# Two trunk layers: state-space tables begun inside the prologue, the first gate vector on TensorE, a pause in the modulation

## The chip, the cores and the metric

The kernel runs on one core of one Trainium2 chip. The metric is the device time of one execution in microseconds, taken as the median over runs; the profile is one further execution of the same program, recorded by the hardware profiler. The engines are TensorE (PE, with its weight loads as PEld), VectorE (DVE), ScalarE (ACT), GpSimd (POOL) and SyncE (SP), which here only starts transfers.

## The reference

Five blocks of 128 tokens (128 context tokens, 512 latent tokens) of width 1024 go through two layers. Cut to what matters here:

```python
def trunk_layer(h, cond, p, ctx):
    m = modulation(cond, p["w_mod"], p["b_mod"])          # silu(cond) @ w_mod + b_mod, 9 vectors of 1024
    sh1, sc1, g1, sh2, sc2, g2, sh3, sc3, g3 = [m[:, :, j] for j in range(N_MOD)]
    x = rmsnorm(h, p["norm_ffn1"]) * (1 + sc1) + sh1
    h = h + 0.5 * g1 * swiglu(x, p["ffn1_w_gate"], p["ffn1_w_up"], p["ffn1_w_down"])
    x = rmsnorm(h, p["norm_mix"]) * (1 + sc2) + sh2
    mixed, new_ctx = token_mixing(x, p, ctx)              # S5 scan | banded attention | axial attention | DFT
    h = h + g2 * mixed
    x = rmsnorm(h, p["norm_ffn2"]) * (1 + sc3) + sh3
    h = h + 0.5 * g3 * swiglu(x, p["ffn2_w_gate"], p["ffn2_w_up"], p["ffn2_w_down"])
```

swiglu is silu(x @ wg) * (x @ wu) @ wd with a hidden width of 2816. The S5 part of token_mixing needs, from parameters alone, the powers of a = exp(lambda dt) and matrices made of b and c; these are the "SSM tables". All of it is float32.

## The kernel before

**Work and tiling.** h is held transposed (`hT`, channels on the partitions) in two halves: half 0 has 256 columns (context and the first latent block), half 1 has 384. A float32 product is made of three matmuls on split operands: `whi` (a rounded copy of the weights, ACT, L205) and `wlo` (the rest, DVE, L206), `xh` and `xl` likewise for x. So a weight slab `raw` of 1 MB costs a transfer on SP's queue (L188), two ACT and two DVE operations, and then three matmuls for each 128 x 128 block.

**Prologue.** `load_x` loads the tokens and starts the first modulation slabs: shift sh1 and scale sc1 are wanted before anything else. `first_load(q)` starts two transfers of 1 MB (`wf`) for quarter q = 0 to 3 of scale (gi = 1) and shift (gi = 0); `first_mod(q)` multiplies each on PE (`macc`, L403, 8 instructions, each recorded twice in the trace's counts), copies it on ACT (`mev`, L406), transposes it on PE with a small matmul (`mpt`, L409) and adds the bias on DVE (`modT`, L411). Then `x_prep` makes xh and xl of blocks k = 2q and 2q + 1 (DVE L550 and L554, ACT L553, L557 and L559, POOL L560). The four of these rounds are called stages here, q0 to q3.

**First feed-forward part (FFN1).** Its hidden blocks f0 and f1 are computed together, k by k as x becomes ready (L663 to L665, 192 matmuls, called "the first 192" here); all later blocks go one at a time through `mm3` (L257 to L259), first gate and up (`gu`), then down (`y`). The residual is L592.

**Work beside it.** Two side streams are fed in by a count of modelled TensorE time, `tick`. (1) The rest of the modulation: `mod_step` makes one 512 KB slab (`wm`, started from POOL's queue, L347) into a partial sum with four DVE operations (`mvec`, L374 and L376); every four steps the partial sum is finished on PE (`macc` L422, four instructions), copied (`mev` L425) and transposed (`mpt` L432, two). Eight steps, so two such sums, make one vector of 1024; steps 0 to 15 would be those that the prologue makes in the other way, so the stream begins with steps 16 to 23 (the first gate g1) within 40 us of counted time, and steps 24 to 71 follow within 300 us. Two `wm` buffers rotate. (2) `ssm_tables`, a generator whose pieces are taken one by one: three pieces that only start 15 small transfers (`lamn`, `ldt`, `bn`, `cn`, `dcol`, `eye`), one with transposes on PE (`pl` L758, `pb` L764, `pc` L771), then many small DVE operations (`z`, `apow`, `eb`), transposes `ebT` (L952) and products `zt` (L973).

**What sets the order.** A scheduler fixes the order of each engine's instructions when the program is built; each engine then runs its own list in that order and waits at the first instruction whose operands are missing. Short-lived tiles (`mev`, `xt`, `rbs`, `lamn`, `cn`, `sg`, `hx`) share one pool of 5 buffers (tag "t"), and the two `rbs` tiles (the row factors) hold two of them through the prologue. By the waits in that order, a transfer of SP's queue starts when the eighth one before it has landed.

**Mixer entry.** At the end of FFN1 the squares of h are summed (`sq`, DVE L575; `pss`, PE L583), turned into 1/rms (`ms`, DVE L511; `rst`, POOL L512), spread over the partitions (`diag`, DVE L522; `rb`, PE L525), and x of the mixer is made from it in two halves. Half 0's S5 input is `pu`, the projections are `pj` (L1010 to L1012).

Of the kernel before, what the change touches and what calls it, by code (L numbers as in the profile page):

```python
# [36 lines left out]
T_OUT = 6500  # L37
FIN = 5
JOB_N = 2500
JOB_D = 12000  # L40
M_LAG = 3000
M_P0 = 40
M_P1 = 300
M_P2 = 340
X_PAT = ("dbdbdbdb", "dbbdbbdb")
LEAD = 2
# [59 lines left out]
class Net:  # L106
# [245 lines left out]
    def mod_step(self):  # L352


        nc = self.nc
        i = self.m_use
        if i == self.m_limit and self.mod_then:
            self.mod_to(*self.mod_then)
            self.mod_then = None
        if i >= min(len(self.mseq), self.m_limit):  # L360
            return
        self.m_use += 1
        l, gi, k = self.mseq[i]
        self.mod_load(i + 1)
        slab = self.mslab.pop(i)
        kk = k % 4
        if kk == 0:
            self.mvec = self.modp.tile([P, 2, 512], F32, name="mvec", tag="mvec")
        for j in range(2):
            w = slab[:, j * 512:(j + 1) * 512]  # L370
            for v in range(2):
                c = self.cs[:, 2 * kk + j, v:v + 1]
                if kk == 0 and j == 0:
                    nc.vector.tensor_scalar(self.mvec[:, v], w, c, None, op0=OP.mult)  # L374
                else:
                    nc.vector.scalar_tensor_tensor(self.mvec[:, v], w, c, self.mvec[:, v], op0=OP.mult, op1=OP.add)  # L376
        self.mod_load(i + 1 + self.mod_bufs)
        if kk == 3:
            mv = self.mvec
            self.later(M_LAG, lambda: self.mod_sum(l, gi, k // 4, mv))  # L380
        if not self.m_pace:
            self.tick(0)
# [33 lines left out]
    def mod_sum(self, l, gi, h, mv):  # L416
# [8 lines left out]
        nc.scalar.activation(ev[:, 0:256], acc, AF.Copy)  # L425
        self.later(900, lambda: self.mod_fin2(l, gi, h, ev))

    def mod_fin2(self, l, gi, h, ev):
        nc = self.nc
        pt = self.b([P, 2, P], name="mpt")  # L430
        for q in range(2):
            nc.tensor.transpose(pt[:, q, :], ev[:, q * P:(q + 1) * P], self.ident)  # L432
        src = pt.rearrange("p q (v s m) -> p v s q m", v=2, s=2)
        k0 = gi * 8 + h * 4
        dst = self.modT[l][:, k0:k0 + 4, :].rearrange("p (s q) v -> p s q v", s=2)
        bias = self.bmod[:, l, k0:k0 + 4].rearrange("p (s q) -> p s q", s=2)
        for v in range(2):
            nc.vector.tensor_tensor(dst[:, :, :, v], src[:, v, :, :, 0], bias, op=OP.add)
        if h == 1:
            self.mod_done(l, gi)  # L440

    def mod_to(self, n, ns=None):

        self.m_limit = n
        if ns is not None:
            self.m_pace = ns / max(n - self.m_use, 1)
            self.m_ns = self.m_pace
            return
        self.m_pace = None
        while self.m_use < n:  # L450
            self.mod_step()
# [26 lines left out]
    def load_x(self):  # L478
        nc, a = self.nc, self.a
        self.rs_tok = self.per.tile([P, 5], F32, name="rs_in", tag="rst", bufs=2)  # L480
        ss = self.per.tile([P, 5], F32, name="ss_in", tag="ss", bufs=2)
        xin = [self.xp.tile([P, w // P, D], F32, name=f"xin{i}", tag=f"xh{i}") for i, (_, w) in enumerate(HALVES)]
        junk = self.xp.tile([P, 2, D], F32, name="sqj", tag="xl0")
        xt = [xin[0][:, i] for i in range(2)] + [xin[1][:, i] for i in range(3)]
        for i in range(5):
            src = a["x_prompt"][0] if i == 0 else a["x_sample"][0, (i - 1) * P:i * P, :]
            nc.sync.dma_start(out=xt[i], in_=src)
        vecs = self.setup_vectors()
        next(vecs)
        self.load_limit = 2  # L490
        self.first_load(0)
        self.load_upto(2)
        self.first_load(1)
        for i in range(5):
            nc.scalar.activation(junk[:, i % 2], xt[i], AF.Square, accum_out=ss[:, i:i + 1])
            half = 0 if i < 2 else 1
            c0 = (i * P) - HALVES[half][0]
            for q in range(2):
                pt = self.b([P, 4, P], name="xT")
                for s in range(4):  # L500
                    nc.tensor.transpose(pt[:, s, :], xt[i][:, (4 * q + s) * P:(4 * q + s + 1) * P], self.ident)
                self.evac(self.hT[half][:, 4 * q:4 * q + 4, c0:c0 + P], pt)
        self.rstd_from(ss[:, 0:5], 0, 5)
        for _ in vecs:
            pass
# [1221 lines left out]
def build(tc, a, depth=DEPTH):  # L1727
    n = Net(tc, a, depth)
    nc = n.nc
    with ExitStack():  # L1730
# [14 lines left out]
        e_pro, pro = n.open_pool("pro", side="right")  # L1745
        n.open_ring_b()
        n.open_modp(2)
        n.load_x()
        rb = [n.norm_bc(h) for h in range(2)]
        for q in range(4):  # L1750
# [2 lines left out]
            n.first_mod(q)  # L1753
            for h in range(2):
                n.x_prep(h, 0, 0, rb[h], range(2 * q, 2 * q + 2))
        n.load_limit = n.seg[0][1]
        n.job = n.ssm_tables(pro, 0)
        n.job_ns = JOB_D
        n.e_mod.close()
        n.prep_to(4)  # L1760
# [1 line left out]
        for l in range(depth):  # L1762
            last = l + 1 == depth
            for j in (0, 2):
# [5 lines left out]
                    n.job = n.ssm_tables(pro, tab)  # L1770
                if l == 0 and j == 0:
                    n.mod_to(24, M_P0 * 1e3)
                    n.mod_then = (72, M_P1 * 1e3)
                else:
                    n.mod_to(min(72 * l + (72 if j == 0 else 96), 72 * depth), M_P2 * 1e3)
                n.ffn(l, j, (l, 1) if j == 0 else ((None, None) if last else (l + 1, 0)), chunks,
# [37 lines left out]
```

## Time and profile before

| | us |
|---|---|
| median of 3 runs (lowest, highest) | 2590.75 (2590.13, 2592.15) |
| the profiled execution: its time | 2590.19 |
| the profiled execution: its span | 2588.3 |
| PE busy | 2521.3 |
| DVE busy | 1499.7 |
| ACT busy | 831.6 |
| POOL busy | 375.4 |

Busy time counts every instruction but those that only branch, wait or start a transfer. The span runs from the first to the last instruction of the record; the 1.9 us between it and the execution's time lie around it. In rows of the timeline, the first number is the start, the second the duration, and the bracket behind a row says how long the engine had been idle and what it waited for; "SPq" rows are issues of transfers, in which the queue may wait too.

### The profile page before, as it was taken

Reading aid. Unit: us, or ns where it says so; the run is one execution under the profiler, and the core shown is the slowest. Engines: PE = TensorE matmul, PEld = TensorE weight load, DVE = VectorE, ACT = ScalarE, POOL = GpSimd, SP = SyncE. Lnnn points to the kernel's source line nnn. Section 1 sums busy time; section 2 is a strip of 40 time slices with the busy share of each in tenths; the row PEclk is TensorE's granted clock in tenths of the full one; section 3 lists DMA queues with packets and bytes.
Section 4 is the critical chain, followed back from the end, with each engine's and each line's share of the span. In section 5 each row is a group of like instructions: output and inputs, shape, how many; then the busy total and the mean of one; then the engine's idle time right before and its main releaser. Section 6 shows DMA issues by size and latency. Waiting matters only on the chain.

```text
span 2588.3 us, 41614 instructions
## 1 busy us (share of the span) xinstructions
PE 2521.3 (97%) x17082; PEld 2375.1 (92%) x17082; DVE 1499.7 (58%) x3014; ACT 831.6 (32%) x1570; POOL 375.4 (15%) x775
## 2 busy tenths in 40 slices
PE   7899999999899999999999999999999999999998
PEld 5799999998679899999999999999876799999998
DVE  5888676353667876454456666644446773333333
ACT  5232222242453532222233222223425553222222
POOL 2122010015701211000011001000183010000000
PEclk8899999999899999999999999999999999999999
DMA  8556454231104254343314445432401133221311
GB/s 270 151 172 192 137 156 146 90 98 55 37 26 147 66 168 127 109 126 98 115 50 152 134 127 153 136 100 66 125 19 54 34 99 98 68 84 62 98 49 41
DMA packets 205253, 273.94 MB, mean 106 GB/s; under 512 B 17224, under 2 KB 176680, under 8 KB 204552
## 3 DMA queue, kind: packets, MB, share of 16 engines
q1 hardware_dynamic: 183048, 193.30, 23.4%
q0 software_dynamic: 22016, 78.00, 10.0%
q8 instruction: 134, 2.20, 0.4%
q14 instruction: 55, 0.45, 0.1%
HBM read 256.29 MB, written 14.97 MB: 105 GB/s over the span
## 4 chain that ended last, share of the span: by engine, by line
PE 77%; issue 8%; POOL 7%; DVE 6%; DMA 2%; ACT 1%; SPq 0%; DVEq 0%; POOLq 0%; ACTq 0%
PE gu L257 14%; PE gu L259 14%; PE gu L258 14%; PE y L257 8%; PE y L258 8%; PE y L259 8%; POOL ee L1124 2%; POOL sc L1121 2%; POOL ee L1123 1%; POOL sc L1122 1%; DVE wlo L206 1%; DVE xt L550 1%; PE macc L422 1%; PE pj L1010 1%; PE pj L1011 1%
## 5 line engine op out<-in xcount | busy, mean ns | idle before, releaser
L257 PE MATMUL gu<-xh,whi 128*128 128x256 f32 (+1 forms) x2560 | 793.2, 310 | 0.9 <-DVE hx L676 0.9
L259 PE MATMUL gu<-xh,wlo 128*128 128x256 f32 (+1 forms) x2560 | 788.6, 308 | 0.6 <-DVE wlo L206 0.6
L258 PE MATMUL gu<-xl,whi 128*128 128x256 f32 (+1 forms) x2560 | 787.8, 308 | 0.0
L205 ACT ACTIVATE whi<-raw 128x1024 fp32r<-128x1024 f32 (+2 forms) x344 | 328.6, 960 | 881.5 <-PE gu L258 435.2
L206 DVE TENSOR_TENSOR wlo<-raw,whi 128x1024 fp32r<-128x1024 f32 (+2 forms) x344 | 377.0, 1098 | 347.3 <-ACT whi L205 346.8
L257 PEld LDWEIGHTS gu<-xh,whi 128*128 128x128 f32 x2560 | 480.6, 188 | 12.3 <-issue 10.2
L258 PEld LDWEIGHTS gu<-xl,whi 128*128 128x128 f32 x2560 | 481.7, 188 | 1.3 <-issue 1.2
L259 PEld LDWEIGHTS gu<-xh,wlo 128*128 128x128 f32 x2560 | 481.0, 188 | 2.0 <-issue 1.2
L257 PE MATMUL y<-hh,whi 128*128 128x384 f32 (+1 forms) x1408 | 435.6, 311 | 0.0
L259 PE MATMUL y<-hh,wlo 128*128 128x384 f32 (+1 forms) x1408 | 434.8, 309 | 0.0
L258 PE MATMUL y<-hl,whi 128*128 128x384 f32 (+1 forms) x1408 | 434.6, 309 | 0.1
L376 DVE SCALAR_TENSOR_TENSOR mvec<-wm,cs,mvec 128x512 f32<-128x512 f32 x448 | 316.7, 746 | 22.1 <-DMA wm<-in_w_mod_dram 21.7
L592 DVE SCALAR_TENSOR_TENSOR hT<-y,G,hT 128x128 f32<-128x128 f32 (+1 forms) x432 | 175.5, 436 | 229.1 <-PE y L259 228.9
L257 PEld LDWEIGHTS y<-hh,whi 128*128 128x128 f32 x1408 | 266.4, 190 | 3.3 <-issue 2.9
L258 PEld LDWEIGHTS y<-hl,whi 128*128 128x128 f32 x1408 | 267.5, 190 | 0.4 <-DVE hl L678 0.3
L259 PEld LDWEIGHTS y<-hh,wlo 128*128 128x128 f32 x1408 | 267.2, 190 | 0.0
L347 POOL DMA_DIRECT2D wm<-in_w_mod_dram x128 | 92.0, 718 | 939.4 <-DVE mvec L376 800.0
L676 DVE TENSOR_TENSOR hx<-sg,gu 128x256 f32<-128x256 f32 (+1 forms) x176 | 85.0, 483 | 121.4 <-ACT sg L674 121.1
L677 ACT ACTIVATE hh<-hx 128x256 fp32r<-128x256 f32 (+1 forms) x176 | 82.8, 471 | 187.4 <-DVE hx L676 187.3
L512 POOL TENSOR_TENSOR rst<-ms,mhalf 128x2 f32<-128x2 f32 (+1 forms) x12 | 11.2, 932 | 855.7 <-DVE ms L511 855.7
L674 ACT ACTIVATE sg<-gu 128x256 f32<-128x256 f32 (+1 forms) x176 | 75.3, 429 | 183.3 <-PE gu L259 176.5
L678 DVE TENSOR_TENSOR hl<-hx,hh 128x256 fp32r<-128x256 f32 (+1 forms) x176 | 86.2, 492 | 51.2 <-ACT hh L677 50.9
(311 smaller groups left out, 3238.4 us busy)
## 6 DMA issues: line engine op xcount, KB each, us to landing
wm<-in_w_mod_dram POOLq DMA_DIRECT2D x128, 512.0 KB, 4.1
raw<-in_ffn_w_gate_dram SPq DMA_DIRECT2D x44, 1024.0 KB, 5.4
raw<-in_ffn_w_up_dram SPq DMA_DIRECT2D x44, 1024.0 KB, 5.1
raw<-in_ffn_w_down_dram SPq DMA_DIRECT2D x24, 1024.0 KB, 5.1
raw<-in_ffn_w_down_dram SPq DMA_DIRECT2D x16, 768.0 KB, 4.6
raw<-in_w_in_dram SPq DMA_DIRECT2D x12, 1024.0 KB, 5.2
wf<-in_w_mod_dram SPq DMA_DIRECT2D x8, 1024.0 KB, 10.7
raw<-in_ffn_w_down_dram SPq DMA_DIRECT2D x16, 512.0 KB
```

The costliest lines, as they stand in the source:

```text
L205: self.nc.scalar.activation(hv, v, AF.Copy)
L206: self.nc.vector.tensor_tensor(lv, v, hv, op=OP.subtract)
L257: self.nc.tensor.matmul(out, wh, xh, start=(i == 0), stop=False)
L258: self.nc.tensor.matmul(out, wh, xl, start=False, stop=False)
L259: self.nc.tensor.matmul(out, wl, xh, start=False, stop=(i == n - 1))
L347: self.nc.gpsimd.dma_start(out=t.rearrange("p (j c) -> p j c", j=2), in_=w[kk * 256:(kk + 1) * 256, c0:c0 + 512].rearrange("(j p) c -> p j ...
L376: nc.vector.scalar_tensor_tensor(self.mvec[:, v], w, c, self.mvec[:, v], op0=OP.mult, op1=OP.add)
L592: nc.vector.scalar_tensor_tensor(h, y[:, s:e], G[:, k, v:v + 1], h, op0=OP.mult, op1=OP.add)
L674: nc.scalar.activation(sg[:, 0:w], g, AF.Silu)
L676: nc.vector.tensor_tensor(hx[:, 0:w], sg[:, 0:w], u, op=OP.mult)
L677: nc.scalar.activation(hh[half][:, f, :], hx[:, 0:w], AF.Copy)
L678: nc.vector.tensor_tensor(hl[half][:, f, :], hx[:, 0:w], hh[half][:, f, :], op=OP.subtract)
```

## The change

Three edits. **(a)** The table generator is created ahead of `load_x`. Its three pieces of transfers are issued right behind `first_load(1)`, its transposes behind stage q2, its next piece behind stage q3, and the first later piece is due after 5000 instead of 12000 counted ns. **(b)** Steps 16 to 23 of the modulation (`M_PE = 24`) are made on PE: 8 matmuls per step accumulate 128 columns each in one PSUM buffer over four steps (`macc`, L375 of the new program), then one copy, one transpose and one DVE addition (`mod_fin1`). **(c)** Steps 24 to 71 are spread over 360 instead of 300 counted us, and the first of them is due 60 us later (`M_D1`). At the end of FFN1 the line `n.mod_to(n.m_limit)` runs, as before, what is left of the steps.

```diff
--- before.py
+++ after.py
@@ -37,10 +37,12 @@
 T_OUT = 6500
 FIN = 5
 JOB_N = 2500
-JOB_D = 12000
+JOB_D = 5000
 M_LAG = 3000
 M_P0 = 40
-M_P1 = 300
+M_P1 = 360
+M_D1 = 60
+M_PE = 24
 M_P2 = 340
 X_PAT = ("dbdbdbdb", "dbbdbbdb")
 LEAD = 2
@@ -364,6 +366,22 @@
         self.mod_load(i + 1)
         slab = self.mslab.pop(i)
         kk = k % 4
+        if i < M_PE:
+            if kk == 0:
+                self.macc = self.b([P, P], name="macc")
+            for j in range(2):
+                for t in range(4):
+                    c0 = j * 512 + t * P
+                    nc.tensor.matmul(self.macc[32 * t:32 * t + 32, :], self.cs[:, 2 * kk + j, :], slab[:, c0:c0 + P],
+                                     start=(kk == 0 and j == 0), stop=(kk == 3 and j == 1), skip_group_check=True)
+            self.mod_load(i + 1 + self.mod_bufs)
+            if kk == 3:
+                ev = self.t(P, "mev")
+                nc.scalar.activation(ev[:, 0:P], self.macc, AF.Copy)
+                self.later(900, lambda: self.mod_fin1(l, gi, k // 4, ev))
+            if not self.m_pace:
+                self.tick(0)
+            return
         if kk == 0:
             self.mvec = self.modp.tile([P, 2, 512], F32, name="mvec", tag="mvec")
         for j in range(2):
@@ -425,6 +443,17 @@
         nc.scalar.activation(ev[:, 0:256], acc, AF.Copy)
         self.later(900, lambda: self.mod_fin2(l, gi, h, ev))
 
+    def mod_fin1(self, l, gi, h, ev):
+        nc = self.nc
+        pt = self.b([P, P], name="mpt")
+        nc.tensor.transpose(pt, ev[:, 0:P], self.ident)
+        src = pt.rearrange("p (t m) -> p t m", t=4)
+        k0 = gi * 8 + h * 4
+        nc.vector.tensor_tensor(self.modT[l][:, k0:k0 + 4, :], src[:, :, 0:2],
+                                self.bmod[:, l, k0:k0 + 4, None].to_broadcast([P, 4, 2]), op=OP.add)
+        if h == 1:
+            self.mod_done(l, gi)
+
     def mod_fin2(self, l, gi, h, ev):
         nc = self.nc
         pt = self.b([P, 2, P], name="mpt")
@@ -439,12 +468,12 @@
         if h == 1:
             self.mod_done(l, gi)
 
-    def mod_to(self, n, ns=None):
+    def mod_to(self, n, ns=None, delay=0):
 
         self.m_limit = n
         if ns is not None:
             self.m_pace = ns / max(n - self.m_use, 1)
-            self.m_ns = self.m_pace
+            self.m_ns = self.m_pace + delay
             return
         self.m_pace = None
         while self.m_use < n:
@@ -491,6 +520,8 @@
         self.first_load(0)
         self.load_upto(2)
         self.first_load(1)
+        for _ in range(3):
+            next(self.job)
         for i in range(5):
             nc.scalar.activation(junk[:, i % 2], xt[i], AF.Square, accum_out=ss[:, i:i + 1])
             half = 0 if i < 2 else 1
@@ -1745,6 +1776,7 @@
         e_pro, pro = n.open_pool("pro", side="right")
         n.open_ring_b()
         n.open_modp(2)
+        n.job = n.ssm_tables(pro, 0)
         n.load_x()
         rb = [n.norm_bc(h) for h in range(2)]
         for q in range(4):
@@ -1753,8 +1785,9 @@
             n.first_mod(q)
             for h in range(2):
                 n.x_prep(h, 0, 0, rb[h], range(2 * q, 2 * q + 2))
+            if q >= 2:
+                next(n.job)
         n.load_limit = n.seg[0][1]
-        n.job = n.ssm_tables(pro, 0)
         n.job_ns = JOB_D
         n.e_mod.close()
         n.prep_to(4)
@@ -1770,7 +1803,7 @@
                     n.job = n.ssm_tables(pro, tab)
                 if l == 0 and j == 0:
                     n.mod_to(24, M_P0 * 1e3)
-                    n.mod_then = (72, M_P1 * 1e3)
+                    n.mod_then = (72, M_P1 * 1e3, M_D1 * 1e3)
                 else:
                     n.mod_to(min(72 * l + (72 if j == 0 else 96), 72 * depth), M_P2 * 1e3)
                 n.ffn(l, j, (l, 1) if j == 0 else ((None, None) if last else (l + 1, 0)), chunks,
```

Three places in the order of instructions follow, of before and then of the changed program (whose line numbers are higher by 2 to 31).

SP's queue in the prologue, up to the transfers of stages q2 and q3 (`wf` x4), before:

```order
L188 DMA raw<-in_ffn_w_up_dram 128x8x256
L390 DMA wf<-in_w_mod_dram 128x8x256 x2
L732 DMA ldt<-in_ssm_log_dt_dram 64x16 x2
L751 DMA dcol<-in_ssm_d_dram 16x4x1 x4
L755 DMA eye_737<-in_k_eye_dram 128x16
L390 DMA wf<-in_w_mod_dram 128x8x256 x4
L188 DMA raw<-in_ffn_w_gate_dram 128x8x256
```

The same place after the change:

```order
L408 DMA wf<-in_w_mod_dram 128x8x256 x2
L758 DMA lamn<-in_ssm_lambda_re_dram 16x2x64
L758 DMA lamn<-in_ssm_lambda_im_dram 16x2x64
L763 DMA ldt<-in_ssm_log_dt_dram 64x16 x2
L769 DMA bn<-in_ssm_b_re_dram 16x2x1024
L769 DMA bn<-in_ssm_b_im_dram 16x2x1024
L775 DMA cn<-in_ssm_c_re_dram 128x2x64 x2
L775 DMA cn<-in_ssm_c_im_dram 128x2x64 x2
L782 DMA dcol<-in_ssm_d_dram 16x4x1 x4
L786 DMA eye_177<-in_k_eye_dram 128x16
L408 DMA wf<-in_w_mod_dram 128x8x256 x4
L190 DMA raw<-in_ffn_w_gate_dram 128x8x256
```

The `wf` x4 of stages q2 and q3 stood behind seven small transfers and now stands behind fifteen.

ACT's list in the prologue, before: `mev_394` is the second of stage q2 (`mev_378` stands just ahead of it), `mev_433` and `mev_449` to q3, `whi_637` and `whi_643` are the first copies of the gate and up slabs of f2 and f3:

```order
L406 ACTIVATE mev_394<-macc_385 128x256
L553 ACTIVATE xh0_284<-xt_400,modT0_96 128x128 x2
L557 ACTIVATE xt_407<-xt_407,modT0_96 128x128 x2
L557 ACTIVATE xt_414<-xt_414,modT0_96 128x384
L559 ACTIVATE xh0_284<-xt_407 128x256
L559 ACTIVATE xh1_300<-xt_414 128x384
L557 ACTIVATE xt_419<-xt_419,modT0_96 128x384
L406 ACTIVATE mev_433<-macc_424 128x256
L205 ACTIVATE whi_637<-raw_483 128x1024
L559 ACTIVATE xh1_300<-xt_419 128x384
L406 ACTIVATE mev_449<-macc_440 128x256
L205 ACTIVATE whi_643<-raw_489 128x1024
```

After the change `mev_400` and `mev_416` belong to q2, and `whi_832` and `whi_838` are those same copies:

```order
L590 ACTIVATE xh0_306<-xt_375 128x256
L588 ACTIVATE xt_382<-xt_382,modT0_96 128x384
L590 ACTIVATE xh1_322<-xt_382 128x384
L207 ACTIVATE whi_832<-raw_596 128x1024
L207 ACTIVATE whi_838<-raw_602 128x1024
L584 ACTIVATE xh1_322<-xt_387,modT0_96 128x384
L424 ACTIVATE mev_400<-macc_391 128x256
L424 ACTIVATE mev_416<-macc_407 128x256
L584 ACTIVATE xh0_306<-xt_422,modT0_96 128x128 x2
```

The copies of the f2 and f3 slabs stood among the evacuations of q3 and now stand ahead of those of q2.

DVE's list at the mixer entry, from the last squares to the x of half 1, before:

```order
L575 TENSOR_TENSOR sq_5069<-sq_5069,sqt 128x384 x2
L511 TENSOR_SCALAR ms<-pss 128x3
L522 TENSOR_SCALAR diag<-ident,rst 128x128 x3
L1591 TENSOR_SCALAR sink<-sink 128x4
L161 COPY uT<-pu 128x32x8
L550 SCALAR_TENSOR_TENSOR xt<-hT_71,A_2562,rbs 128x384 x4
```

And after the change:

```order
L606 TENSOR_TENSOR sq_4983<-sq_4983,sqt 128x384 x2
L542 TENSOR_SCALAR ms<-pss 128x3
L392 TENSOR_SCALAR mvec<-wm,cs 128x512 x2
L394 SCALAR_TENSOR_TENSOR mvec<-wm,cs,mvec 128x512 x14
L163 COPY uT<-pu 128x32x8
L553 TENSOR_SCALAR diag<-ident,rst 128x128 x3
L581 SCALAR_TENSOR_TENSOR xt<-hT_71,A_3363,rbs 128x384 x2
```

Sixteen `mvec` operations, those of the last four modulation steps, stand between `ms` and `diag`; on PE, the 8 `macc` of the last two sums stand directly ahead of `rb`, and five more `mvec` stand among the operations of the 30 rows before these.

## Rows read from the trace of the kernel before

**Rows 1.** The profile page: busy time of each engine, its share, instructions.

```profile
PE 2521.3 (97%) x17082; PEld 2375.1 (92%) x17082; DVE 1499.7 (58%) x3014; ACT 831.6 (32%) x1570; POOL 375.4 (15%) x775
```

**Rows 2.** Windows: stretch, length, busy time by engine, PEclk, DMA share, GB/s.

```profile
16.00:32.00 16.00, 11.32 (x63) 6.00 (x66) 8.28 (x16) 8.65 (x16) 1.65 (x1) 0.52 1.10 347
32.00:36.00 4.00, 4.00 (x24) 3.19 (x17) 0.00 (x0) 0.38 (x1) 2.70 (x3) 0.50 0.29 53
...
116.00:120.00 4.00, 3.15 (x16) 1.63 (x16) 3.18 (x7) 0.61 (x2) 0.00 (x0) 0.50 0.61 212
400.00:500.00 100.00, 100.00 (x691) 97.92 (x690) 51.05 (x84) 27.84 (x46) 4.24 (x6) 1.00 0.36 112
560.00:620.00 60.00, 58.78 (x358) 52.92 (x357) 26.16 (x45) 23.10 (x44) 14.74 (x28) 1.00 0.30 86
```

**Rows 3.** Timeline of SP's queue in the prologue.

```profile
33.97 5.23 SPq L390 DMA_DIRECT2D wf<-in_w_mod_dram  x4
39.25 2.91 SPq L188 DMA_DIRECT2D raw<-in_ffn_w_gate_dram  x1
```

**Rows 4.** Transfers of the page and of 64 to 72 us: count, KB, us to landing.

```profile
wm<-in_w_mod_dram POOLq DMA_DIRECT2D x128, 512.0 KB, 4.1
...
cn<-in_ssm_c_re_dram SPq DMA_DIRECT2D x2, 64.0 KB, 4.1
```

**Rows 5.** Timeline of ACT in the prologue.

```profile
23.16 0.38 ACT L406 ACTIVATE mev<-macc 128x256 f32<-128x256 f32 x1 [3.00 <-PE macc L403]
...
27.96 2.00 ACT L205 ACTIVATE whi<-raw 128x1024 fp32r<-128x1024 f32 x2 [0.58 <-DMA raw<-in_ffn_w_up_dram]
...
43.07 0.38 ACT L406 ACTIVATE mev<-macc 128x256 f32<-128x256 f32 x1
...
51.94 1.06 ACT L205 ACTIVATE whi<-raw 128x1024 fp32r<-128x1024 f32 x1 [0.94 <-DMA raw<-in_ffn_w_gate_dram]
...
53.32 0.36 ACT L406 ACTIVATE mev<-macc 128x256 f32<-128x256 f32 x1
54.92 1.06 ACT L205 ACTIVATE whi<-raw 128x1024 fp32r<-128x1024 f32 x1 [1.24 <-DMA raw<-in_ffn_w_up_dram]
```

**Rows 6.** Timeline of PE from stage q3 to the first `y`.

```profile
51.65 1.07 PE L403 MATMUL macc<-wf,cs 128*32 128x256 f32 x16
...
53.92 0.50 PE L409 MATMUL mpt<-sel,mev 128*128 128x2 f32 x4
...
79.96 1.94 PE L764 MATMUL pb<-ident,bn 32*128 32x32 f32 x16 [3.58 <-DMA bn<-in_ssm_b_im_dram]
...
83.02 0.56 PE L257 MATMUL gu<-xh,whi 128*128 128x256 f32 x1
...
116.74 0.66 PE L952 MATMUL ebT<-ident,eb 128*128 128x128 f32 x2 [4.72 <-DVE eb L923]
...
118.35 1.54 PE L952 MATMUL ebT<-ident,eb 128*128 128x128 f32 x6
...
121.53 0.56 PE L257 MATMUL y<-hh,whi 128*128 128x256 f32 x1
...
132.09 0.56 PE L973 MATMUL zt<-rt,bb 128*32 128x240 f32 x5 [0.96 <-DVE hT L592]
```

**Rows 7.** Timeline of DVE: `mvec` operations back to back.

```profile
72.80 2.74 DVE L376 SCALAR_TENSOR_TENSOR mvec<-wm,cs,mvec 128x512 f32<-128x512 f32 x4
...
321.58 0.88 DVE L374 TENSOR_SCALAR mvec<-wm,cs 128x512 f32<-128x512 f32 x2 [3.10 <-PE macc L422]
```

**Rows 8.** Timeline of DVE and PE at the mixer entry.

```profile
539.21 0.62 DVE L592 SCALAR_TENSOR_TENSOR hT<-y,G,hT 128x384 f32<-128x384 f32 x1 [1.61 <-PE y L259]
...
556.63 0.16 DVE L511 TENSOR_SCALAR ms<-pss 128x3 f32<-128x3 f32 x1 [0.92 <-PE pss L583]
557.76 0.68 DVE L522 TENSOR_SCALAR diag<-ident,rst 128x128 f32<-128x128 f32 x3 [0.97 <-POOL rst L512]
...
559.37 0.81 PE L525 MATMUL rb<-diag,ones 128*128 128x384 f32 x2
```

## The prediction

> **What bounds the kernel now.** The page's list of busy times comes first: PE works 2521.3 us of a span of 2588.3 [rows 1]. So whatever delays PE's list costs its full length, and whatever DVE, ACT or a queue saves counts only where PE stands behind it. The windows then show which stretches these are. In steady FFN1 (400 to 500 us) PE is busy 100.00 of 100 us at a granted clock of 1.00, and DVE only 51.05 [rows 2]: edits to DVE's work there are worth nothing. In the prologue the transfers bind: from 16 to 32 us the DMA engines move 347 GB/s at a share of 1.10, with one hole from 32 to 36 us at 53 GB/s, and PE's clock is 0.50 to 0.52, the lower of its two levels [rows 2]. Between 65 and 132 us PE stands 3.58 us for `bn`, 4.72 for `eb`, 0.96 for `hT` [rows 6], and about 3.3 in three shorter waits beside them, after which it runs at half clock (0.50 from 116 to 120 us, [rows 2]). With the time lost at half clock these come to some 19 us; that is the most that the prologue edits can win. The mixer entry is the third stretch: `ms`, `diag` and `rb` follow one another on three engines, and 2.7 us pass from `ms` to `rb`, covered on PE by the last 24 `pu` matmuls [rows 8].
>
> **(a) Tables early: SP's queue.** Before, the `wf` of stages q2 and q3 are issued at 33.97 [rows 3], when the second `wf` of q1 has landed. After, eight small transfers more stand ahead. The eighth ahead of the `wf` of q2 is now the second `cn`, and the eighth ahead of that is the `wf` of q1. So the queue goes through two landings in a row: 33.97 + 4.1 (a `cn` takes 4.1 us, [rows 4]) + 0.1 = 38.2. All behind it moves by 4.2 us: the gate slab of f2 and f3, whose copy starts on landing at 51.94, lands at about 56.2, the up slab (54.92) at 59.1 [rows 5].
>
> **(a) Tables early: ACT's list.** This is the larger part. An engine waits at the first instruction that is not ready: `mev` of q3 at 53.32 already stands behind the copy that waits for a slab at 51.94 [rows 5]. After the change two such places are worse. The copies of the first up slab (ready at 27.96, two in 2.00 us) stand ahead of the second `mev` of q0, which was at 23.16: it moves to 30.0 [rows 5], and the first 192 start near 33.4 instead of 26.4. And both copies of the f2 and f3 slabs stand ahead of the `mev` of q2, which were at 43.07 and later [rows 5]. With the slab at 59.1, 1.06 for the copy, one `xh` and the `mev`, q2's first `mpt` comes at 59.1 + 1.06 + 0.6 + 0.4 + 1.3 (queueing and signals) = 62.5. PE by then has done all that its list holds ahead of it (by my count of the list, 48 of the 192 and the sums of q1 and q2), at about 52.2: it idles some 10 us and continues at half clock.
>
> From q2's first `mpt` on I follow the list: second `mpt` 65.9; `pl`, `pb` and `pc` to 69.7 (their 16 `pb` took 1.94 us at half clock, [rows 6]); sum of q3 70.4; q3's `mpt` 74 and 77.5. Each round from `mev` to `x` is serial, since `lamn`, `cn` and the two `rbs` leave one of the five "t" buffers to rotate; I allow 3.5 us for one, where q3 before took from 51.65 to 53.92 [rows 6] with more buffers. At 77.5 there are 120 of the 192 left; before, at 53.92 [rows 6], there were 124. At 100 us for 691 of the same mixture [rows 2], 0.145 each, 120 take 17.4 us.
>
> **(b) The gate on PE.** Not shown in before: a step of 8 matmuls of 128 columns. Bounds: half of L403's 1.07 us for 8 of 256 columns [rows 6], so 0.54, or by the count alone 1.07; 8 steps cost 4.3 to 8.6 us, and what goes with it (two sums of about 0.6 and four `mpt`) returns 2. I take the columns, since L403 is the nearest row, the same instruction on the same operands with twice the columns. It takes 32 `mvec` operations off DVE, 28 of 0.66 and 4 of 0.40 us [rows 7], 20 us. DVE is what `eb` waits for, so the stall of 4.72 shrinks, to an estimated 1.2. In its place PE waits for the slabs: `wm` takes 4.1 us to land [rows 4], two buffers rotate, and the first four steps stand within 10 us of PE's list; I count 1.6 us.
>
> So up to f2: 77.5 + 0.4 + 17.4 + 2.2 (four steps) + 1.6 + 1.2 + 1.6 (`ebT`, [rows 6]) + 0.8 (a fifth step, `mpt`) = 102.7, against 83.02 before [rows 6]: +19.7. From there to `y`, before takes 38.5 us with the stall of 4.72 in it; after takes 27.8 for 192 matmuls, 1.6 for three steps, 1.0 `zt`, 1.6 `ebT`, 0.3: 32.3, so `y` starts at 135.0 against 121.53 [rows 6], +13.5. Before then still has 5.1 us to pay that after has paid: 2.2 at half clock, 0.96 of waiting, 1.02 for `zt` [rows 6], 1.0 for the rest. **Prologue: +8.4**, with bounds of -8 (each round 1.5 us shorter, evacuations not held behind the slab) and +16 (1.07 per step, a landing waited for at each slab).
>
> The Trainium skill, "DMA: Bandwidth & Descriptors", section "Rules for kernel authors", advises to issue a transfer early and to wait for it late, so that its fixed cost lies under compute; by that rule alone edit (a) wins the 3.58 us of `bn` and its half clock. The same table warns that transfers under 64 KB are mostly overhead, which speaks against fifteen of them at this place; the row of 4.1 us for 64 KB beside 4.1 for 512 agrees [rows 4].
>
> **(c) The pause.** Steps of 7.5 counted us after a first one at 67.5 end at 40 + 67.5 + 47 x 7.5 = 460 counted us (457.5 by the counts at which they begin); FFN1 counts about 431. Four steps are left over, and their 16 `mvec` stand between `ms` and `diag`. Their price: 2 x 0.40 + 14 x 0.66 = 10.1 us [rows 7]; the `wm` of the last two are only issued when the first two have freed their buffers, 0.7 + 4.1 us [rows 4] behind 2.6, which adds 1.8: 11.9. The cover is the 2.8 us of `pu`, which already covers `rst` and `diag`, so nothing is left of it. `rb` moves from 559.37 [rows 8] to about 570.5, +11.1. Then the two sums and `rb` run at half clock after 11 idle us, as at 116 to 120 [rows 2], which I put at 1.4: +12.5. Five more `mvec`, 3.3 us, stand ahead of x of half 0, where DVE idles 1.61 [rows 8] and 0.3: +1.4. **Mixer: +13.9**, bounds 9 (no slab waited for, half the clock loss) and 17 (both slabs in full). Nothing behind it takes this back: from 560 to 620 PE is busy 58.78 of 60 us [rows 2]. What it frees earlier, fewer `mvec` at a time in FFN1, is worth nothing, as above.
>
> **Sum.** 2590.2 + 8.4 + 13.9 = 2612.5 for the profiled execution; the median of the runs lies 0.56 above it: **2613**.
>
> **Rivals.**
> - The leftover steps cost as above, but the prologue breaks even, since the evacuations get past the slabs sooner than I count and the stalls for `bn` and `eb` go: 2590.75 + 13.9 = 2604.7.
> - The prologue wins what it is after. All 19.2 us of standing and half clock between 65 and 132 come back, less 2.6 of gate work on PE: -16.6. With the mixer at +13.9 the time is 2588, within the bound.
> - The other side: the same -16.6, and the leftover steps cost no more than 9, since slabs are ready and DVE had idle time: 2590.75 - 7.6 = 2583. It decides once the `mev` of q2 come before about 50 us; against it stands ACT's list.
> - PE waits in addition for single slabs, 4.1 us each [rows 4], at three of the first steps: 2613 + 12 = 2625.
> - The change does nothing: ruled out by the order, which puts sixteen operations in front of `diag`.
>
> **How the numbers follow.** Main case 0.55, break-even prologue 0.18, prologue won 0.10, other side 0.07, slabs waited for 0.10. The range of 2594 to 2629 leaves out the two cases that end near or below the old time (0.17) and little above. A measurement tells 0.2%, 5.2 us, from no change. Faster by more than that: the other side and half of the third case, 0.12. Within: the other half and a trace of the second, 0.07. Slower: 0.81.
>
> **What the profile after would show.** SP's `wf` of q2 near 38; ACT's `mev` of q2 near 62 behind two `whi`, and PE idle about 10 us ahead of it at a clock of 0.50; the first `mm3` matmul near 103 and the first `y` near 135; no wait for `bn`; sixteen `mvec` between `ms` and `diag` in 10 to 13 us and an `rb` some 12 us later after `ms` than now; nothing new from 150 us to there, nor behind it. The prediction is wrong if `mev` of q2 comes before 50 us, if the gate steps take 1.07 us or wait for slabs, or if the delay of `rb` is made up before the scan.

## The result and the profile after

The changed kernel takes 2629.1 us (median of 4 runs, 2628.04 to 2629.88) against 2591.45 of the kernel before beside it: ratio 1.0137, 95% interval 1.0111 to 1.0162, so some 29 to 42 us slower. The forecast was 2613, slower, with a range to 2629: the time stands at the range's upper end (by the ratio to the 2590.75 that the forecast started from it would be 2626). The profiled execution has a span of 2626.9, 38.6 above that of before.

Where the time went is read by following one mark of the program after another. `pss` of half 0, just ahead of the mixer, starts 11.3 us later than before; `ms` of half 1 15.1 later (556.63 before, [rows 8]); `rb` of half 1 34.3 later (559.37). From the prologue's end to that `pss` PE is as full as before (100.00 of 100 us at clock 1.00 from 400 to 500), and what lies behind `rb` adds 4 us, of which more below. So there are two places, the two that were forecast.

**The prologue.** Windows of before, from the first modulation matmul to 75 us and from there to 135 (columns as in [rows 2]):

```profile
14.00:75.00 61.00, 51.72 (x356) 40.38 (x357) 39.18 (x87) 27.05 (x58) 17.31 (x16) 0.83 0.85 266
75.00:135.00 60.00, 49.30 (x320) 45.54 (x321) 52.01 (x168) 14.93 (x34) 10.57 (x12) 0.86 0.49 150
```

The same windows after:

```profile
14.00:75.00 61.00, 42.28 (x219) 27.66 (x220) 23.86 (x69) 21.36 (x43) 12.05 (x10) 0.53 0.73 224
75.00:135.00 60.00, 55.35 (x486) 51.44 (x486) 44.25 (x142) 19.96 (x45) 15.85 (x23) 0.97 0.56 170
```

The eighth column is the granted clock: 0.83 before, 0.53 after. PE has 219 matmul records in the first stretch where it had 356, and spent nearly all of it at the lower level (0.50 from 40 to 60 us, where before had 1.00 from 38 to 60). In the second stretch it does better than before (486 for 320, clock 0.97 for 0.86). SP's queue, and behind it ACT's list, in the timeline after (answering to [rows 3] and [rows 5]):

```profile
38.18 9.93 SPq L408 DMA_DIRECT2D wf<-in_w_mod_dram  x4
...
26.50 2.00 ACT L207 ACTIVATE whi<-raw 128x1024 fp32r<-128x1024 f32 x2 [1.00 <-DMA raw<-in_ffn_w_up_dram]
28.41 0.36 ACT L424 ACTIVATE mev<-macc 128x256 f32<-128x256 f32 x1
...
56.48 1.06 ACT L207 ACTIVATE whi<-raw 128x1024 fp32r<-128x1024 f32 x1 [1.31 <-DMA raw<-in_ffn_w_gate_dram]
59.34 1.06 ACT L207 ACTIVATE whi<-raw 128x1024 fp32r<-128x1024 f32 x1 [1.80 <-DMA raw<-in_ffn_w_up_dram]
...
62.29 0.39 ACT L424 ACTIVATE mev<-macc 128x256 f32<-128x256 f32 x1 [1.39 <-DVE xl L585]
```

`wf` of q2 at 38.18, the slabs of f2 and f3 at 56.48 and 59.34, the `mev` of q2 behind both at 62.29: each within half a microsecond of the forecast. The `mev` had one more wait, which the forecast did not have: 1.39 us for an `xl`. It reads nothing of it; the tile that it writes is of the pool of five that `xt` and `mev` share. PE's list shows what stood behind them (answering to [rows 6]):

```profile
28.83 1.01 PE L427 MATMUL mpt<-sel,mev 128*128 128x2 f32 x4 [5.93 <-ACT mev L424]
38.43 0.58 PE L696 MATMUL gu<-xl,whi 128*128 128x256 f32 x1 [4.50 <-POOL xl L591]
...
60.95 0.69 PE L694 MATMUL gu<-xh,whi 128*128 128x384 f32 x1 [2.99 <-ACT xh L584]
...
92.63 0.65 PE L375 MATMUL macc<-wm,cs 128*32 128x128 f32 x16 [1.52 <-DMA wm<-in_w_mod_dram]
96.40 0.69 PE L694 MATMUL gu<-xh,whi 128*128 128x384 f32 x1 [3.13 <-DVE hx L707]
...
107.91 0.38 PE L259 MATMUL gu<-xh,whi 128*128 128x256 f32 x1
...
139.91 0.28 PE L259 MATMUL y<-hh,whi 128*128 128x256 f32 x1
...
545.67 0.50 PE L614 MATMUL pss<-ones,sq 128*128 128x1 f32 x4
```

There is no single long hole. PE waits three times between 20 and 75 us, 5.93, 4.50 and 2.99 us, and in between it works through its few matmuls at 0.21 us each for 256 columns, where it took 0.12 in before at a clock of 1.00. The first matmul of f2 starts at 107.91 and the first `y` at 139.91 (83.02 and 121.53 before, [rows 6]). `pss` of half 0, here at 545.67, stood in the timeline of before at:

```profile
534.40 0.50 PE L583 MATMUL pss<-ones,sq 128*128 128x1 f32 x4
```

**The mixer entry.** DVE after, from `ms` of half 1 to `diag` (answering to [rows 8]):

```profile
571.76 0.16 DVE L542 TENSOR_SCALAR ms<-pss 128x3 f32<-128x3 f32 x1 [1.41 <-PE pss L614]
577.88 0.88 DVE L392 TENSOR_SCALAR mvec<-wm,cs 128x512 f32<-128x512 f32 x2 [5.96 <-PE macc L440]
578.68 4.06 DVE L394 SCALAR_TENSOR_TENSOR mvec<-wm,cs,mvec 128x512 f32<-128x512 f32 x6
587.10 5.39 DVE L394 SCALAR_TENSOR_TENSOR mvec<-wm,cs,mvec 128x512 f32<-128x512 f32 x8 [4.37 <-DMA wm<-in_w_mod_dram]
...
592.84 0.65 DVE L553 TENSOR_SCALAR diag<-ident,rst 128x128 f32<-128x128 f32 x3
```

1.1 us lay between `ms` and `diag` before, 21.1 lie there now, 10.3 of them operations and 10.3 two waits. The slab of the second wait was asked for by POOL at 580.38, behind the first `mvec` that freed a buffer:

```profile
580.38 0.75 POOL L349 DMA_DIRECT2D wm<-in_w_mod_dram  x1 [7.50 <-DVE mvec L394]
```

PE meanwhile:

```profile
570.40 1.32 PE L614 MATMUL pss<-ones,sq 128*128 128x1 f32 x6 [2.21 <-DVE sq L606]
...
576.99 0.82 PE L440 MATMUL macc<-mvec,ones 128*32 128x256 f32 x8
591.98 1.64 PE L440 MATMUL macc<-mvec,ones 128*32 128x256 f32 x8 [14.18 <-DVE mvec L394]
593.64 1.62 PE L556 MATMUL rb<-diag,ones 128*128 128x384 f32 x2
```

It stands for 14.18 us, and behind that `rb` takes 1.62 where it took 0.81 in before [rows 8], at a clock of 0.50 from 592 to 594 us. (The 1.64 of the second `macc` beside the 0.82 of the first measures no clock: its later matmuls wait for the last `mvec`, which ends at 592.49.) The clock was low ahead of that hole too: the 24 `pu` between `pss` and the first `macc` took 5.4 us at 0.50 (572 to 577 us), where they took 2.9 in before. The window from 560 to 620, 58.78 us busy at clock 1.00 in [rows 2], is now 43.59 us busy at 0.80:

```profile
560.00:620.00 60.00, 43.59 (x280) 40.58 (x279) 35.10 (x65) 20.06 (x40) 12.50 (x12) 0.80 0.37 112
```

### The profile page after: what moved, and what is told of

Read it like the earlier page. It is cut to its first block, busy times and chain, and to the rows that moved or that the text cites. A ratio compares the mean times of both kernels' runs of the same rounds, so it can differ in the third digit from the quotient of the medians.

```text
span 2626.9 us, 41784 instructions
## 1 busy us (share of the span) xinstructions
PE 2540.3 (97%) x17192; PEld 2389.7 (91%) x17192; DVE 1484.3 (57%) x2980; ACT 834.3 (32%) x1570; POOL 377.4 (14%) x775
## 3 DMA queue, kind: packets, MB, share of 16 engines
q8 instruction: 135, 2.21, 0.3%
## 4 chain that ended last, share of the span: by engine, by line
PE 75%; issue 9%; POOL 7%; DVE 5%; DMA 2%; ACT 1%; SPq 1%; DVEq 0%; POOLq 0%; ACTq 0%
PE gu L259 14%; PE gu L261 14%; PE gu L260 14%; PE y L259 7%; PE y L260 7%; PE y L261 7%; POOL ee L1155 2%; POOL sc L1152 2%; POOL ee L1154 1%; POOL sc L1153 1%; DVE wlo L208 1%; DVE xt L581 1%; PE pj L1041 1%; DMA wm<-in_w_mod_dram 1%; PE pj L1042 1%
## 5 line engine op out<-in xcount | busy, mean ns | idle before, releaser
L261 PE MATMUL gu<-xh,wlo 128*128 128x384 f32 (+1 forms) x2560 | 788.8, 308 | 0.6 <-DVE wlo L208 0.6
L260 PE MATMUL gu<-xl,whi 128*128 128x384 f32 (+1 forms) x2560 | 787.0, 308 | 0.0
L394 DVE SCALAR_TENSOR_TENSOR mvec<-wm,cs,mvec 128x512 f32<-128x512 f32 x420 | 297.8, 748 | 27.5 <-DMA wm<-in_w_mod_dram 27.1
```

The source lines that it names most:

```text
L260: self.nc.tensor.matmul(out, wh, xl, start=False, stop=False)
L261: self.nc.tensor.matmul(out, wl, xh, start=False, stop=(i == n - 1))
```

## The experiments

Ratios are to the kernel before, each with its 95% interval. 0.0010 is 2.6 us.

**Each edit alone.** The other two are undone. (a) alone:

```diff
-M_P1 = 360
-M_D1 = 60
-M_PE = 24
+M_P1 = 300
+M_D1 = 0
+M_PE = 0
```

> Edit (a) alone: the tables begin in the prologue; the gate stays on VectorE, the modulation has the old pace. Theory 1 (the prologue's loss of some 11 us belongs to (a), because ScalarE's list puts slab copies ahead of the evacuations of q0 and q2): 10 to 15 us slower than before, 2601 to 2606. Theory 2 (the loss comes from the gate matmuls of (b) and their waits for slabs): within 4 us of before, 2587 to 2595.

2622.75 us, 1.0102 (1.0081 to 1.0123): 21 to 32 us slower, twice what theory 1 gave and far from theory 2. The prologue goes as in the changed kernel, and one wait more comes in. PE:

```profile
108.00 0.69 PE L694 MATMUL gu<-xh,whi 128*128 128x384 f32 x1 [19.42 <-DVE hx L707]
```

PE stands 19.42 us for one `hx`: DVE has the gate's `mvec` and the tables' operations to do ahead of it, since both begin in the same stretch. In the changed kernel this wait is 3.13, because (b) has taken the `mvec` away.

(b) alone:

```diff
-M_P1 = 360
-M_D1 = 60
+M_P1 = 300
+M_D1 = 0
...
-        n.job = n.ssm_tables(pro, 0)
         n.load_x()
...
+        n.job = n.ssm_tables(pro, 0)
         n.job_ns = JOB_D
```

(with the lines that step the tables in the prologue taken out, and JOB_D = 12000).

> Edit (b) alone: the gate on TensorE, tables and pace as before. Theory 1: 20 us of VectorE work leave the stretch in which TensorE waits for eb, and 4.3 us of matmuls come: 0 to 5 us faster than before, 2586 to 2591. Theory 2: 6 to 12 us slower, 2597 to 2603.

2580.47 us, 0.9942 (0.9925 to 0.9960): faster by 10 to 19 us, more than theory 1 gave; theory 2 is out. Its windows:

```profile
14.00:75.00 61.00, 52.10 (x416) 40.23 (x417) 29.83 (x73) 27.26 (x59) 17.65 (x17) 0.86 0.90 278
75.00:135.00 60.00, 58.56 (x452) 55.02 (x452) 53.10 (x170) 18.27 (x36) 12.76 (x16) 1.00 0.54 170
```

From 75 to 135 us PE is busy 58.56 us at a clock of 1.00 where before it was busy 49.30 at 0.86: the waits for `bn` and `eb` are gone, and with them the half clock.

(c) alone, with the tables as in the last diff:

```diff
-M_PE = 24
+M_PE = 0
```

> Edit (c) alone: pace 360 with a pause of 60 counted us, so that four steps are left at the end of the first feed-forward part. Theory 1 (the sixteen operations between ms and diag, with their waits, hold up the mixer's entry): 22 to 26 us slower than before, 2613 to 2617. Theory 3 (the mixer's loss comes from elsewhere, as the later start of its tables' tail or of the transfers): under 12 us slower, below 2603.

2618.68 us, 1.0089 (1.0072 to 1.0106), 19 to 27 us slower, so theory 1's 22 to 26 and not theory 3. DVE at the mixer's entry repeats the rows above:

```profile
558.60 0.16 DVE L540 TENSOR_SCALAR ms<-pss 128x3 f32<-128x3 f32 x1 [1.53 <-PE pss L612]
564.52 0.88 DVE L392 TENSOR_SCALAR mvec<-wm,cs 128x512 f32<-128x512 f32 x2 [5.77 <-PE macc L440]
...
573.68 5.39 DVE L394 SCALAR_TENSOR_TENSOR mvec<-wm,cs,mvec 128x512 f32<-128x512 f32 x8 [4.30 <-DMA wm<-in_w_mod_dram]
```

The three add up: 1.0102 + 0.9942 + 1.0089 - 2 = 1.0133, beside 1.0137 for all together.

**The pause without left-over steps.** All three edits, but the steps fit:

```diff
-M_P1 = 360
+M_P1 = 310
```

> All three edits, but with a pace of 310 in place of 360, so that the last step falls inside the first feed-forward part and no modulation operation is left at the mixer's entry. Theory 1: the mixer's 24 us are back and the prologue's 11 to 13 stay: 2602 to 2606. Theory 3: it stays above 2615.

2608.57 us, 1.0051 (1.0034 to 1.0067). 0.0086 of the 0.0137 comes back, 22 us, near what theory 1 gave and far from theory 3: the left-over steps cost that, and not the pause. What stays is (a) and (b), 9 to 17 us.

**Fewer left-over steps.** A pace of 340, with no operation left between `ms` and `diag` of half 1. By its trace sixteen `mvec` stand between `ms` of half 0 and `ms` of half 1 (I had counted ten near the entry), where the changed kernel has five there and sixteen behind:

```diff
-M_P1 = 360
+M_P1 = 340
```

> All three edits, with a pace of 340 in place of 360: ten modulation operations still stand near the mixer's entry, but none between ms and diag. If the price is that of operations standing in that chain with their waits: 2606 to 2613, near the version whose pause fits. If every left-over operation costs its time wherever it stands at the entry: 2616 to 2622.

2617.24 us, 1.0096 (1.0072 to 1.0120), the runs spread from 2612.60 to 2626.69. The median is in the second alternative's range, but the interval reaches into the first's, so the time alone does not decide. The trace does: operations outside that chain cost too. From `ms` of half 0 to that of half 1 DVE is the engine that sets the pace, and PE waits for an `xl` that stands behind `mvec`:

```profile
570.44 0.58 PE L260 MATMUL pu<-xl,whi 128*128 128x256 f32 x1 [4.76 <-DVE xl L585]
```

```profile
545.00:577.00 32.00, 25.03 (x145) 23.57 (x145) 29.66 (x61) 14.99 (x33) 6.84 (x8) 0.86 0.42 133
```

The window has 29.66 of 32 us busy on DVE, 25.03 on PE. The price is that of the entry as a whole.

**What of (a) loses: buffers or queue.** First the buffers: (b) alone, and two of the five short-lived tiles taken from `load_x` to behind stage q2, without any transfer or transpose:

```diff
+        for w in [128, 512]:
+            h_ = self.t(w, "held")
+            nc.gpsimd.memset(h_[:, 0:w], 0.0)
+            self.held.append(h_)
...
+            if q == 2:
+                for i_, h_ in enumerate(n.held):
+                    n.nc.vector.tensor_tensor(n.held_out[:, i_:i_ + 1], h_[:, 0:1], n.modT[0][:, 4:5, 0], op=OP.add)
```

> Edit (b) alone, with the tables as before, but two of the five short-lived buffers are held by two tiles (filled by a memset on GpSimd, read after stage q2): no transfer and no transpose is moved. Theory 1a (the early tables lose because lamn and cn hold two buffers, which makes the rounds serial and puts slab copies ahead of evacuations): it loses most of what (a) loses beside (b), 15 to 28 us over (b) alone, 2596 to 2608. Theory 1b (they lose because fifteen transfers stand ahead of the wf of q2 and q3 on SP's queue): within 4 us of (b) alone, 2577 to 2585.

2592.67 us, 0.9997 (0.9982 to 1.0012): the whole gain of (b) is gone, some 14 us by the ratios, a little under theory 1a's 15 to 28 and far from theory 1b's 4. The order that comes out has the slab copies ahead of the evacuations of q2, though no transfer was moved. ACT:

```profile
51.65 1.06 ACT L207 ACTIVATE whi<-raw 128x1024 fp32r<-128x1024 f32 x1 [1.93 <-DMA raw<-in_ffn_w_gate_dram]
54.66 1.06 ACT L207 ACTIVATE whi<-raw 128x1024 fp32r<-128x1024 f32 x1 [1.44 <-DMA raw<-in_ffn_w_up_dram]
55.62 0.36 ACT L424 ACTIVATE mev<-macc 128x256 f32<-128x256 f32 x1
```

Then the queue: (b) alone, and fifteen transfers of a constant into a tile of their own, at the place of the tables' fifteen:

```diff
+        extra = self.extra.tile([P, 15, 16], F32, name="extra")
+        for i in range(15):
+            nc.sync.dma_start(out=extra[:, i, :], in_=a["k_eye16"])
```

> Edit (b) alone, with fifteen small transfers of a constant into a tile that nothing reads, issued where the change issues the table transfers: the first wf of q2 then waits for the eighth transfer before it as in the changed kernel, and no buffer is held. It tells the queue's share of what (a) loses beside (b), 28 us, from the buffers' share, of which two held buffers showed 12. If the queue carries the rest: 12 to 18 us over (b) alone, 2592 to 2599. If it only moves wf by some 4 us, which stage q2 passes on: 2 to 7 us over (b) alone, 2582 to 2588, and the rest comes from the two together.

2581.00 us, 0.9948 (0.9931 to 0.9965), beside 0.9942 of (b) alone: no loss that can be told in the time, and the first alternative, 12 to 18 us, is out. The trace does show a few microseconds. The first `wf` of q2 moved by 3.3 (33.94 with (b) alone), the first evacuation of q2 by 2.3 (42.79 there), and PE waited 3.74 for that `wf`, where its longest wait for a `wf` with (b) alone is 0.8:

```profile
23.53 13.62 SPq L525 DMA_DIRECT2D extra<-in_k_eye_dram  x15
37.25 0.38 SPq L408 DMA_DIRECT2D wf<-in_w_mod_dram  x1
...
45.06 0.38 ACT L424 ACTIVATE mev<-macc 128x256 f32<-128x256 f32 x1 [2.56 <-PE macc L421]
```

```profile
43.01 1.94 PE L421 MATMUL macc<-wf,cs 128*32 128x256 f32 x16 [3.74 <-DMA wf<-in_w_mod_dram]
```

f2 starts 3.7 us later than with (b) alone (81.94, 78.25) and `pss` of half 0 4.5 later (526.23, 521.69). So the queue's shift is worth some 4 us at the mixer's entry, within the second alternative's 2 to 7, and about a third of what two held buffers cost. Then (a) and (b) with one buffer given back:

```diff
-        lamn = self.t(P, "lamn")
+        lamn = pro.tile([P, P], F32, name="lamn")
```

> Edits (a) and (b), old pace, with lamn in a tile of its own, so that one short-lived buffer less is held and ScalarE's list has the evacuations of q2 ahead of the slab copies again (those of q0 and q3 still stand behind copies). If the order of ScalarE's list is the main carrier: 10 to 18 us of the loss come back, 2590 to 2599. If one buffer more or less is worth little: 2603 to 2609, as (a) and (b) together.

2590.25 us, 0.9986 (0.9977 to 0.9995), against 1.0044 for (a) and (b) by their sum (1.0102 + 0.9942 - 1; the two alone at the old pace are not among the runs): 15 us back, in the range that was given for the order of ScalarE's list. The `mev` of q2 stand ahead of the copies again, and the second `mev` of q0 still stands behind them:

```profile
28.40 0.36 ACT L424 ACTIVATE mev<-macc 128x256 f32<-128x256 f32 x1
...
45.29 0.38 ACT L424 ACTIVATE mev<-macc 128x256 f32<-128x256 f32 x1 [1.22 <-PE macc L421]
51.33 0.38 ACT L424 ACTIVATE mev<-macc 128x256 f32<-128x256 f32 x1 [5.65 <-PE macc L421]
56.38 1.05 ACT L207 ACTIVATE whi<-raw 128x1024 fp32r<-128x1024 f32 x1
```

What is still lost beside (b) alone, some 11 us, stands in PE's waits: 7.26 us behind q0's `mev` (the longest there with (b) alone is 3.46), 3.23 for the `wf` of q2, and 6.10 for an `hx` that stands in DVE's list behind the tables' operations (none with (b) alone):

```profile
28.82 1.01 PE L427 MATMUL mpt<-sel,mev 128*128 128x2 f32 x4 [7.26 <-ACT mev L424]
...
83.24 0.69 PE L694 MATMUL gu<-xh,whi 128*128 128x384 f32 x1 [6.10 <-DVE hx L707]
```

Two variants put the transfers elsewhere. From POOL's queue, at the old pace; each of the six issuing lines of the tables is edited like this:

```diff
-            nc.sync.dma_start(out=lamn[ri * NG:(ri + 1) * NG, 0:P].rearrange("g (d p) -> g d p", d=2),
+            nc.gpsimd.dma_start(out=lamn[ri * NG:(ri + 1) * NG, 0:P].rearrange("g (d p) -> g d p", d=2),
```

> Edits (a) and (b), old pace, with the fifteen table transfers issued from GpSimd's queue, so that SP's wf stand where they stood or earlier. Theory 1a: it stays 10 to 16 us slower than before, 2602 to 2609, since the buffers are held and ScalarE's list is as in the changed kernel. Theory 1b: it falls to (b) alone, 2577 to 2585.

2615.37 us, 1.0077 (1.0052 to 1.0103). That is in neither theory's range and settles nothing on SP's queue. The transfers now stand ahead of POOL's `pow` for the row factors (`rs_in`), which starts at 18.86 (13.64 in before), and in DVE's list `diag` of the row factors has fallen behind two `wlo`, which wait for ACT's copies of the first slab. PE waits for that `diag`:

```profile
29.00 2.36 DVE L208 TENSOR_TENSOR wlo<-raw,whi 128x1024 fp32r<-128x1024 f32 x2 [10.57 <-ACT whi L207]
...
31.90 1.19 PE L556 MATMUL rb<-diag,ones 128*128 128x256 f32 x2 [14.60 <-DVE diag L553]
```

And behind stage q2, at the old pace:

```diff
-        for _ in range(3):
-            next(self.job)
...
+            if q == 2:
+                for _ in range(3):
+                    next(n.job)
             if q >= 2:
                 next(n.job)
```

> Edits (a) and (b), old pace, with the table transfers issued behind stage q2 in place of ahead of q0; transposes follow behind q2 and q3 as in the change. lamn and cn then take their buffers after most evacuations. Theory 1a: 2577 to 2586, the gain of (b) kept, with the wait for bn and its half clock gone or moved. Theory 1b: the transfers still stand ahead of the wf of q2 in part, so 2586 to 2600.

2599.43 us, 1.0019 (1.0003 to 1.0035): 20 us more than (b) alone. That is out of theory 1a's range and at the upper end of theory 1b's, but the evacuations of q2 stand near where they stood before (43.11 and 46.19), so it is another loss than either. The transposes stand in PE's list inside the prologue and wait for the late transfers, and `hx` waits for DVE:

```profile
58.02 0.28 PE L787 MATMUL pl<-ident,lamn 32*128 32x32 f32 x1 [3.45 <-DMA lamn<-in_ssm_lambda_im_dram]
...
86.75 0.69 PE L692 MATMUL gu<-xh,whi 128*128 128x384 f32 x1 [4.17 <-DVE hx L705]
```

**Towards a better version.** (b) with a pause that fits, tables as before:

```diff
-M_P1 = 360
+M_P1 = 310
```

> Edit (b) with the pause of 60 counted us and a pace of 310, so that no step is left over; tables as before. If the modulation's VectorE work stands in the way just behind the prologue, the pause gives 2 to 5 us over (b) alone, 2575 to 2579; if TensorE is full there anyway, nothing within 2 us, 2579 to 2583.

2579.10 us, 0.9937 (0.9915 to 0.9958): not to be told from (b) alone. And (b) with only the due time of (a):

```diff
-JOB_D = 12000
+JOB_D = 5000
```

> Edit (b), with the tables begun behind the prologue as before but their pieces due after 5000 instead of 12000 counted ns (the part of (a) that touches no prologue order). If VectorE, freed of the gate, has room for the tables earlier, the waits for bn and eb shrink: 2573 to 2579. If nothing waits for the tables there any more, within 2 us of (b) alone: 2578 to 2583.

2574.89 us, 0.9928 (0.9912 to 0.9945), the lowest here, 14 to 23 us under before; its interval overlaps that of (b) alone. From 100 to 130 us PE has almost no idle time left (28.56 us busy there with (b) alone):

```profile
100.00:130.00 30.00, 29.96 (x210) 28.84 (x209) 26.68 (x52) 11.45 (x21) 7.21 (x12) 1.00 0.77 251
```

## Why the prediction was right, and where it was too small

Its direction and its two places held, and so did the order of instructions that it built on at both. The size did not: 22.3 us forecast, 38.6 between the two profiled executions. The 16.3 that are missing are 2.9 in the prologue (11.3 for 8.4, within its bounds), 9.1 at the mixer's entry (23.0 for 13.9, outside its bounds of 9 to 17) and 4.3 behind it, where nothing was forecast. The terms, in its own order:

- **SP's queue** ("38.2", "56.2", "59.1"): measured 38.18, 56.48, 59.34. Right as a time; as a cause of loss it carries some 4 us at the mixer's entry by the trace with fifteen constants, and nothing that can be told in that kernel's time. The two landings in a row are shown by the fifteen constant transfers, which moved `wf` in the same way.
- **ACT's list** (q2's `mev` near 62): 62.29. That held buffers bring this order about, and that they cost some 14 us, is shown by the run with two held buffers and, from the other side, by the one with a buffer given back. Whether the loss goes through the order itself or through rounds that have fewer tiles to rotate, no run parts; the wait of 1.39 for `xl` shows the second at work too. Of the 26 us or so that (a) loses, one buffer carries about 15. The rest, some 11, lies with the order at q0, the queue and the tables' operations ahead of `hx` together, and no run parts these.
- **"It idles some 10 us and continues at half clock"**: this step failed in its form. PE was not done with its list at 52.2: it worked until 58.0, since its 48 matmuls took 0.21 or 0.32 us each at the lower clock, and the last six of them waited 2.99 for an `xh` behind the slab copies. The other holes, 5.93 and 4.50 us, lie earlier. What comes out hardly differs, which is luck in part, as a slower PE fills the hole that I had counted as idle: q2's first `mpt` starts at 63.68 for 62.5, q3's second at 79.22 for 77.5. f2 starts at 107.91 in place of 102.7, and of these 5.2 us only 1.7 come from up to here. The others lie behind: 3.13 of waiting for an `hx` that was not in the sum, and 1.3 for nine matmuls at the lower clock behind that wait, less the 1.2 allowed for `eb`.
- **The gate on PE**: a step took 0.65 us by 16 records, between the bounds of 0.54 and 1.07 and nearer to the first; the wait for a slab 1.52 for 1.6; the stall of 4.72 for `eb` is gone altogether. What I had not listed is the wait of 3.13 for `hx`, behind the tables' operations on DVE.
- **Prologue, +8.4**: 11.3 at `pss` of half 0. The first `y` was 18.4 late (13.5 forecast), and behind its own first `y` before lost 7.1 of that again (5.1 forecast). The two misses partly cancel.
- **"Which adds 1.8: 11.9"**, the price of the sixteen operations, is the term that was mis-sized most: `rb` is 19.1 us later behind `ms` than before, for 11.1 in the sum. The operations took 10.3 (10.1 forecast). The slab wait was 4.37, not 1.8: the sum's own terms (0.7 + 4.1 behind 2.6, less some 4.8 for the first eight operations) give 2.6, and the two slabs took 6.2 to 6.6 us from issue to landing in place of the median of 4.1 [rows 4]. And 5.96 us were not in the sum at all: the first `mvec` of a new sum writes the buffer that the `macc` of the sum before still has to read, and these `macc` stand on PE behind the 24 `pu`, which ran at the lower clock. The row at 321.58 in [rows 7] had shown such a wait, 3.10 us. I had counted what stands behind the waiting operations, not what the first of them waits for. A second buffer for the sums was not tried. With all steps inside FFN1 both waits are gone together.
- **"+1.4"** for the five operations ahead of half 0: 3.9 by the marks, from `pss` of half 0 to `ms` of half 1. The idle time that I set against them was not left: DVE is busy 22.41 of the 24 us from 548 to 572, and PE waits 2.21 for the squares of half 1.
- **Nothing behind it**: 4.3 us came behind the start of `rb`. 1.1 of them are added by the end of that mixer, at whose start the clock is still 0.50, 0.5 by the entry of the second layer's, and 2.8 in that second mixer, a stretch that varies in kernels without the change too (last section).

The rivals: the break-even prologue missed by 11 us; the prologue that wins is what (b) does when left alone; slabs waited for at the gate steps came once, 1.52 us, and not at three steps of 4.1, so that rival's 2625 is nearest in time and wrong in its cause. The rule of the Trainium skill to issue a transfer early and wait for it late ("DMA: Bandwidth & Descriptors", section "Rules for kernel authors") has its part in the trace: the changed kernel does not wait for `bn`. But (b) alone does not either, with the transfers where they were, and here the early issue is bought with two of five buffers held from the issue to the read, which cost 14 us without any transfer. The same table's warning against transfers under 64 KB bears on nine of the fifteen (the `bn` are of 128 KB, the `cn` of 64); fifteen of 8 KB in place of the tables' made PE wait 3.74 us for the `wf` behind them, and cost nothing that can be told in the whole.

## What to carry to other kernels

A transfer that is issued early holds its destination until it is read: where a pool rotates few buffers through a serial chain, count them before moving a load ahead of that chain, or give it a tile of its own. A stream of side work that is paced by a count must end inside the stretch that it was laid out for; what is left over lands in the next stretch in front of whatever is short there, together with its buffer waits; so ask of an operation that is put ahead of a chain what it waits for itself. And where PE gets holes, price the matmuls between them at the lower clock, not only the holes.

## What the runs showed of the hardware that was not expected

Behind a wait of 14.18 us on PE `rb` took 1.62 us at a granted clock of 0.50, where it took 0.81 in before. But the clock had been at 0.50 ahead of that wait as well, from 572 to 577 us, behind a wait of 2.21 us and sums of one column (1.00 from 566 to 568). In the prologue three holes of 2.99 to 5.93 us lie in a stretch of sixty in which the clock was 0.53.

A 512 KB slab that lands in 4.1 us by the median took 6.2 to 6.6 at the mixer's entry, where the DMA engines' share was 1.01 (580 to 585 us).

The second layer's mixer varied where nothing was changed. From `ms` of its entry to `ms` of its end the kernel with (b) and fifteen constant transfers took 279.7 us (1812.64 to 2092.33), before 280.7 (1820.75 to 2101.42) and the changed kernel 283.4:

```profile
1856.55 0.16 DVE L542 TENSOR_SCALAR ms<-pss 128x3 f32<-128x3 f32 x1 [0.92 <-PE pss L614]
2139.98 0.15 DVE L542 TENSOR_SCALAR ms<-pss 128x2 f32<-128x2 f32 x1
```

Among the fourteen profiles the stretch lies between 279.7 and 283.9, and kernels with and without (a), and with and without a pause, stand near both ends. The first layer's mixer varies as well, from `rb` at its entry to `rb` at its end between 284.0 and 290.4 (before 285.0, the changed kernel 286.1). What sets either stays open; the second layer's 2.8 are most of the 4.3 us above.
